# A macaron feed-forward block on one core: parts 1 to 3 of each output product by seven block products, with every instruction of the feed-forwards put in order by a list schedule

## The chip, the core and the metric

The kernel runs on one core of one Trainium2 chip. Its time is the device time of one execution in microseconds (us). TensorE (PE in the profile) multiplies 128x128 weight tiles with 128-row activation tiles into PSUM banks; VectorE (DVE) and ScalarE (ACT) do elementwise work; GpSimd (POOL) and SyncE (SP) mostly start transfers here. Weights come from the chip's memory (HBM) into SBUF by DMA. A transfer that SP starts runs on the profile's queue q1, one that POOL starts on q0.

## What is computed

One decoder block on 512 tokens of width 1024, all in float32: a feed-forward, a token mixer (pooling and dilated attention, gated), a second feed-forward, and a last norm. The change lies in the two feed-forwards:

```python
def swiglu(u, w_in, w_out):
    a, b = jnp.split(u @ w_in, 2, axis=-1)
    return (jax.nn.silu(a) * b) @ w_out
...
u = modulate(rmsnorm(h, g_norm_ffn1[l]), sh1, sc1)
h = h + 0.5 * gt1 * swiglu(u, w_ffn1_in[l], w_ffn1_out[l])
...
u = modulate(rmsnorm(h, g_norm_ffn2[l]), sh3, sc3)
h = h + 0.5 * gt3 * swiglu(u, w_ffn2_in[l], w_ffn2_out[l])
```

The inner width is 2816, that is 22 tiles of 128.

## The kernel before

**Three products for one.** Each float32 operand is split into a high part (rounded to float32r) and a low part (the rest). A product is then three matmuls, high x high, high x low and low x high: `mm3` for 512 token columns, `product` for 256. For a weight tile ACT copies the high part into the ring `whi` (L319) and DVE writes the low part into the ring `wlo` (L336). The rings hold 7 chunks of 1024 columns. `look(4)` lets this splitting run up to four products ahead of PE. For the output weights of the second feed-forward the low part is made otherwise (`added`, L333 and L334): ACT writes minus the high part into `wlo`, and a transfer that POOL starts adds the raw weight to it.

**Pairs.** The feed-forward goes over the 22 inner tiles j. Each needs an a column block and a b column block of w_in, 8 tiles of 128x128 each. The first tiles (6 in feed-forward 1, 4 in feed-forward 2) are done plainly. From there `duo` takes two j at a time by Winograd's form of Strassen's scheme: the product of the 2x2 blocked weights (input halves x a and b) and the 2x2 blocked activations (input halves x token halves) takes seven block products of 24 matmuls with 256 columns, where the plain way takes eight. The weight sums that it needs are four DVE subtractions of 1024 columns to a duo, in `make` (L263). The activation sums are made once for each feed-forward. The end of a duo forms silu(a) times b in `hf` (L776) and splits it into `HI` (ACT) and `HK` (DVE, L783).

**Parts.** The 22 inner tiles are cut into five parts, (0,4), (4,8), (8,12), (12,16), (16,22). After a part's tiles, one duo later for most parts, its output product is added to the residual `H`: 8 output tiles of 128 rows by 512 tokens, each 4 inner tiles by three matmuls of 512 columns (`mm3`, L366 to L368), that is 96 matmuls; then DVE adds gate times bank to `H` (L906, 512 columns, eight times). The last part has six inner tiles and its own code, with the norm behind it.

**What sets the order.** Each engine runs its instructions in the order of the program. That order is written by hand: `look` puts splits and loads ahead of a product, `later` and `step` put DVE and ACT work a product or two behind, `bg` puts one slice of the conditioning product in between (a load of 512 KB and a DVE multiply-accumulate of 1024 columns, L393). Feed-forward 1 carries 32 of these slices, 24 of them beside the outputs of its parts 1 to 3.

Of the kernel before, what the change touches and what calls it, by code (L numbers as in the profile page):

```python
# [18 lines left out]
KT = 8  # L19
# [42 lines left out]

def lay_ffn(w_in, w_out, first, plain):

    ins, outs = [], []
    if first:
        cols = np.concatenate([c for j in range(first) for c in _tiles(j * P, DFF + j * P)])
        for k in range(KT):  # L70
            ins.append(w_in[k * P:(k + 1) * P][:, cols])
    for j in range(first, plain):
        for c in _tiles(j * P, DFF + j * P):
            ins.append(_fmajor(w_in, c))
    for j in range(plain, FT, 2):
        ins.extend(_blocks(w_in, 0, DFF, j))
    for k0, k1 in PARTS:
        for m in range(KT):
            outs.append(_fmajor(w_out[k0 * P:k1 * P], np.arange(m * P, (m + 1) * P)))
    n = KT * (len(PARTS) - 1)  # L80
    return ins, [np.concatenate(outs[i:i + 2], axis=1) for i in range(0, n, 2)] + outs[n:]
# [46 lines left out]
NH = 6  # L128
# [5 lines left out]
def pairs_before(n, part):  # L134

    k1 = PARTS[part][1]
    return k1 if part + 1 == len(PARTS) or (n == 2 and part == 0) else k1 + 2


def chunk_widths():  # L140
    outs = [D] * (KT // 2 * (len(PARTS) - 1)) + [(FT - PARTS[-1][0]) * P] * KT
    f1 = [2 * FIRST * P] * KT + [D] * (2 * (FT - FIRST)), outs
    mix = [D] * 24 + [4 * P] * 2 + ([D] * 4 + [4 * P] * 2) * (KT // 2 - 1) + [D] * KT
    return f1, mix, ([D] * (2 * FT), outs)


class Kernel:
# [6 lines left out]
    def plan(self):  # L154
# [12 lines left out]
        self.shifted, self.added = set(), set()  # L167
# [8 lines left out]
        def blocks(recs):  # L176
            n = len(self.loads)
            self.shifted.update(range(len(self.order), len(self.order) + 7))
            self.loads.extend(recs)
            r11, r12, r22, r21 = (("raw", n + i) for i in range(4))  # L180
            x0, x1 = ("x", 0), ("x", 1)
            for need, src, make in ((0, r11, None), (1, x0, (x0, r12, r11)), (2, x1, (x1, r22, x0)), (3, r21, None),
                                    (3, r12, (r12, r22, r12)), (3, r22, None), (3, x0, (x0, r21, x1))):
                for j, x in enumerate((r11, r12, r22, r21)):
                    if x == src or (make and x in make):
                        self.last[n + j] = len(self.order)
                self.order.append((D, n + need, src, make))
# [5 lines left out]
        def ffn(n, ins, outs, first):  # L193
            j, at = first, 0
            if first:
                plain(ins[:KT])
                at = KT
            for part, (k0, k1) in enumerate(PARTS):
                while j < pairs_before(n, part):
                    if j < PLAIN[n]:  # L200
                        plain(ins[at:at + 2])
                        if n and j < 2:
                            shift(2)
                        j, at = j + 1, at + 2
                    else:
                        blocks(ins[at:at + 4])
                        j, at = j + 2, at + 4
                if n and part + 1 < len(PARTS):
                    self.added.update(range(len(self.order), len(self.order) + KT // 2))
                plain(outs[part * KT // 2:(part + 1) * KT // 2] if part + 1 < len(PARTS) else outs[-KT:])  # L210
# [15 lines left out]
        self.ready = True  # L226
# [30 lines left out]
    def make(self, i):  # L257

        while self.made <= i:
            m = self.order[self.made][3]  # L260
            if m:
                out, x, y = (self.source(z) for z in m)
                self.nc.vector.tensor_tensor(out, x, y, op=OP.subtract)  # L263
            self.made += 1

# [28 lines left out]
    def split_hi(self):  # L294
# [15 lines left out]
        self.make(i)  # L310
        r = self.source(self.order[i][2])
# [32 lines left out]
    def look(self, ahead=3):  # L344

        if self.held is not None:
# [23 lines left out]
    def settle(self, bank, hi, uh):  # L370

        self.nc.tensor.matmul(bank[:, :HT - SHIFT], hi, uh[:, SHIFT:HT], start=True, stop=True, skip_group_check=True)

# [26 lines left out]
    def ada_fin(self, which, j0, j1, g=None):  # L400
# [6 lines left out]
        elif which == "half":  # L407
            nc.vector.tensor_scalar(m, m, 0.5, None, op0=OP.mult)

# [26 lines left out]
    def sumsq(self, m, src):  # L436
# [5 lines left out]
        s = self.tp.tile([P, T], F32, name="ut")  # L442
# [25 lines left out]
    def norm_t(self, n, k, hs):  # L468
        G = self.mod[:, 24 * n + 8 + k:24 * n + 9 + k]
        t = self.tp.tile([P, T], F32, name="ut")  # L470
# [97 lines left out]
    def out_end(self, ms, ksrc, gate):  # L568
# [18 lines left out]
        for h, hs in enumerate((A, Bh)):  # L587
            for m in ms:
# [20 lines left out]
                s = self.tp.tile([P, T], F32, name="ut")[:, :HT]  # L609
# [65 lines left out]

    def ffn_post(self, j, s, pb):
        nc = self.nc
        h = self.fw.tile([P, T], F32, name=("hf", "u3")[j % 2])
        nc.vector.tensor_tensor(h, s, pb, op=OP.mult)
        hh, hl = self.HH[j % NH], self.HL[j % NH]  # L680
        nc.scalar.activation(hh, h, AF.Copy)
        nc.vector.tensor_tensor(hl, h, hh, op=OP.subtract)

    def ffn_silu(self, j, pa):
        s = self.fw.tile([P, T], F32, name=("sl", "u2")[j % 2])
# [22 lines left out]
    def u_steps(self, n):  # L708

        nc, v = self.nc, self.nc.vector  # L710
        (a11, a12), (a21, a22) = self.U4

        def add(o, x, y, op):
            return lambda: v.tensor_tensor(o, x, y, op=op)

        def split(i, u):
            x = u if i < 3 else u.rearrange("p (k t) -> p k t", k=4)
            parts = [lambda: nc.scalar.activation(self.S[i][0], x, AF.Copy),
                     lambda: v.tensor_tensor(self.S[i][1], x, self.S[i][0], op=OP.subtract)]
            return parts if n else lambda: [f() for f in parts]  # L720

        def whole(u, k):
            x = slice(k, k + 4)
            hi, lo = (y.rearrange("p (k t) -> p k t", k=KT)[:, x, :HT] for y in (self.UHv, self.ULv))
            return lambda: v.tensor_tensor(u.rearrange("p (k t) -> p k t", k=4), hi, lo, op=OP.add)

        adds = [add(a22, a21, a22, OP.add), add(a21, a11, a21, OP.subtract), add(a11, a22, a11, OP.subtract),
                add(a12, a12, a11, OP.subtract)]
# [13 lines left out]
    def product(self, bank, u, start, extra=0):  # L742
        M = self.nc.tensor.matmul
        w = self.take()
# [10 lines left out]
    def duo(self, n, j, first, last, extra):  # L755
# [12 lines left out]
        s = self.fw.tile([P, 2 * T], F32, name="sl")  # L768
        c = self.fw.tile([P, 2 * T], F32, name="hf")
        u2, u3, p5 = (self.fw.tile([P, T], F32, name=x) for x in ("u2", "u3", "p5"))  # L770
        q = lambda x: x.rearrange("p (j h t) -> p j h t", j=2, h=2)
        r = lambda x: x.rearrange("p (j t) -> p j t", j=2)
        silu = lambda h, bank: nc.scalar.activation(q(s)[:, :, h, :], r(bank), AF.Silu)

        def mult():
            v.tensor_tensor(c, s, c, op=OP.mult)  # L776

        def high():
            copy(self.HHall[:, j % NH * T:(j % NH + 2) * T], c)

        def low():
            x = slice(j % NH * T, (j % NH + 2) * T)
            v.tensor_tensor(self.HLall[:, x], c, self.HHall[:, x], op=OP.subtract)  # L783


        for i, (bank, u, start) in enumerate(((A, blk(lo4, T1), True), (B, S[0], True), (A, S[1], False),
                                              (C, blk(hi4, T1), False), (A, S[2], False), (B, S[3], False),
                                              (A, blk(hi4, T2), False))):
            if i == 6:
                v.tensor_tensor(q(c)[:, :, 1, :], r(u3), r(p5), op=OP.add)  # L790

# [3 lines left out]
            self.product(bank, u, start, 0 if i else extra)  # L795
            self.step()
# [11 lines left out]
            elif i == 3:  # L808
                silu(0, C)
            elif i == 4:  # L810
                copy(u3, A)
            elif i == 6:
                silu(1, A)
                v.tensor_tensor(q(c)[:, :, 0, :], r(B), r(u2), op=OP.add)
        if last:
            mult()
            high()
            low()
        else:
            self.later(1, mult)  # L820
            self.later(2, high)
            self.later(2, low)

    def ffn2(self):
        self.put, self.now = [], 0
        bk = [self.nb() for _ in range(4)]
        self.head(2, bk, AF.Silu)
# [19 lines left out]
    def open_ffn(self):  # L847
# [3 lines left out]
        self.HHall, self.HLall = (fp.tile([P, NH * T], F32R, name=x) for x in ("HI", "HK"))  # L851
        self.HH, self.HL = ([x[:, i * T:(i + 1) * T] for i in range(NH)] for x in (self.HHall, self.HLall))
# [14 lines left out]
    def ffn(self, n, j, last=None):  # L867

        nc, v = self.nc, self.nc.vector
# [7 lines left out]

        for part, (k0, k1) in enumerate(PARTS):
            tail = part + 1 == len(PARTS)
            extra = 1  # L880
            while j < pairs_before(n, part):
# [3 lines left out]
                else:  # L885
                    self.duo(n, j, last, tail and j + 2 == FT, extra)
                    last, extra = None, 0
                    j += 2
            if n == 0:
                last = self.beside_out(part) or last  # L890
            nk = k1 - k0
            hk = [(self.HH[k % NH], self.HL[k % NH]) for k in range(k0, k1)]
            if not tail:
                for m in range(0, KT, 2):
# [8 lines left out]
                    for i, b in enumerate(bs):  # L903
# [5 lines left out]
                        if n == 0 and part:  # L909
                            self.later((6, 13)[i], self.bg) if m + 2 == KT else self.bg()  # L910
# [39 lines left out]
            else:  # L950
                self.out_tail((4, 5, 6, 7), ks, gate, 1, lambda m: self.X[0][:, m % 2 * HT:])

# [25 lines left out]
    def mix_sums(self, x, slots):  # L978
# [17 lines left out]
        sub = lambda o, y, z: v.tensor_tensor(o, y, z, op=OP.subtract)  # L996

        def last():
# [6 lines left out]
        return [lambda: whole(b, 0, 1), lambda: whole(x[0], 4, 1), lambda: v.tensor_tensor(x[0], x[0], b, op=OP.add),  # L1005
                lambda: whole(x[1], 0, 0), lambda: sub(x[2], x[1], b), lambda: sub(x[1], x[0], x[1]),
                lambda: (hi(0), whole(x[3], 4, 0)), lambda: lo(0), lambda: (hi(1), sub(x[3], x[3], x[1])),
# [421 lines left out]
    def gate_duo(self, s, c, p5, last, rest):  # L1429
# [37 lines left out]
        sig(c, c)  # L1467
# [100 lines left out]
    def build(self):  # L1568
# [3 lines left out]
        self.tp = ctx.enter_context(tc.tile_pool(name="tp", bufs=3))  # L1572
# [18 lines left out]
        self.hpi, self.r4 = tl("hpi", 1), tl("r4", 4)  # L1591
# [6 lines left out]
        tl("pad", 32)  # L1598
        self.tr, self.pi = tl("tr", 5 * P), tl("pi", P, I32)
# [3 lines left out]
        self.todo = []  # L1603
# [197 lines left out]
```

## Time and profile before

| what | value |
|---|---|
| time, median of 3 runs | 993.09 us (993.02 to 994.11) |
| span of the profiled execution | 994.0 us, 0.9 us above the median |
| ACT busy | 490.7 us (49%) |
| POOL busy | 45.6 us (5%) |
| memory read / written | 135.29 MB / 2.24 MB |

From the timeline of PE, feed-forward 1 runs from the start to 355 us, the mixer to about 650 us, feed-forward 2 from there to the end. In feed-forward 1 the outputs of parts 1 to 3 stand at 141 to 163, 201 to 223 and 261 to 283 us; in feed-forward 2 at 770 to 792, 830 to 852 and 890 to 912 us. Between them PE does two duos in 38.1 us. A row of the view by lines names line, engine, operation, output<-inputs, shape and count, then the busy time of the group, the mean ns of one, and the idle time of the engine before it with what ended it. A DVE or ACT instruction's own duration is some 0.08 us longer than the distance to the next one, since the two overlap.

### The profile page before, as it was taken

Reading aid. Unit: us, or ns where it says so; the run is one execution under the profiler, and the core shown is the slowest. Engines: PE = TensorE matmul, PEld = TensorE weight load, DVE = VectorE, ACT = ScalarE, POOL = GpSimd, SP = SyncE. Lnnn points to the kernel's source line nnn. Section 1 sums busy time; section 2 is a strip of 40 time slices with the busy share of each in tenths; the row PEclk is TensorE's granted clock in tenths of the full one; section 3 lists DMA queues with packets and bytes.
Section 4 is the critical chain, followed back from the end, with each engine's and each line's share of the span. In section 5 each row is a group of like instructions: output and inputs, shape, how many; then the busy total and the mean of one; then the engine's idle time right before and its main releaser. Section 6 shows DMA issues by size and latency. Waiting matters only on the chain.

```text
span 994.0 us, 16420 instructions
## 1 busy us (share of the span) xinstructions
PE 983.2 (99%) x6688; PEld 894.6 (90%) x6688; DVE 765.0 (77%) x1072; ACT 490.7 (49%) x730; POOL 45.6 (5%) x49
## 2 busy tenths in 40 slices
PE   9999999999999999999999999999999999999997
PEld 7888999989999899788879998998899898998997
DVE  7989979889797677897988877865695775647753
ACT  5453643625434553455555552555366255363553
POOL 0000000000000000007100000001001001010002
PEclk9999999999999999999999999999999999999999
DMA  9856456464564416664233336416454538264312
GB/s 347 275 196 224 149 149 198 146 196 163 188 189 119 126 56 230 201 200 144 76 106 107 106 121 211 135 44 141 128 177 115 142 118 220 86 151 128 114 33 85
DMA packets 47469, 150.14 MB, mean 151 GB/s; under 512 B 6561, under 2 KB 9377, under 8 KB 47394
## 3 DMA queue, kind: packets, MB, share of 16 engines
q1 hardware_dynamic: 44224, 140.18, 43.3%
q0 software_dynamic: 2592, 8.39, 4.6%
q8 instruction: 52, 0.85, 0.3%
q10 hardware_dynamic: 578, 0.53, 0.2%
q14 instruction: 23, 0.19, 0.1%
HBM read 135.29 MB, written 2.24 MB: 138 GB/s over the span
## 4 chain that ended last, share of the span: by engine, by line
PE 89%; DVE 3%; issue 3%; DMA 3%; SPq 1%; ACT 1%; POOL 0%; POOLq 0%; DVEq 0%; ACTq 0%
PE bank L366 14%; PE bank L368 14%; PE bank L367 14%; PE bank L751 13%; PE bank L753 12%; PE bank L752 12%; PE bank L1727 2%; PE bank L1729 1%; PE bank L1731 1%; DMA wlo<-raw 1%; SPq L1059 1%; PE bank L1403 1%; PE bank L1105 1%; PE bank L1156 1%; PE bank L1404 1%
## 5 line engine op out<-in xcount | busy, mean ns | idle before, releaser
L336 DVE TENSOR_TENSOR wlo<-raw,whi 128x1024 fp32r<-128x1024 f32 (+4 forms) x148 | 155.6, 1064 | 53.9 <-ACT whi L319 53.6
L319 ACT ACTIVATE whi<-raw 128x1024 fp32r<-128x1024 f32 (+4 forms) x162 | 146.4, 921 | 63.1 <-DVE raw L263 51.4
L751 PE MATMUL bank<-UH,whi 128*128 128x256 f32 x640 | 177.1, 277 | 0.0
L752 PE MATMUL bank<-UL,whi 128*128 128x256 f32 x640 | 177.1, 277 | 0.0
L753 PE MATMUL bank<-UH,wlo 128*128 128x256 f32 x640 | 177.1, 277 | 0.0
L366 PE MATMUL bank<-HI,whi 128*128 128x512 f32 (+1 forms) x406 | 146.2, 360 | 0.0
L368 PE MATMUL bank<-HI,wlo 128*128 128x512 f32 (+1 forms) x406 | 145.9, 359 | 0.3 <-DMA wlo<-raw 0.3
L367 PE MATMUL bank<-HK,whi 128*128 128x512 f32 (+1 forms) x406 | 145.9, 359 | 0.0
L336 DVE TENSOR_TENSOR wlo<-X,whi 128x1024 fp32r<-128x1024 f32 (+3 forms) x100 | 106.8, 1077 | 22.8 <-ACT whi L319 22.3
L753 PEld LDWEIGHTS bank<-UH,wlo 128*128 128x128 f32 x640 | 120.5, 188 | 0.0
L751 PEld LDWEIGHTS bank<-UH,whi 128*128 128x128 f32 x640 | 120.1, 188 | 0.4
L752 PEld LDWEIGHTS bank<-UL,whi 128*128 128x128 f32 x640 | 120.2, 188 | 0.0
L319 ACT ACTIVATE whi<-X 128x1024 fp32r<-128x1024 f32 (+3 forms) x104 | 96.2, 944 | 45.9 <-DVE X L263 44.5
L751 PE MATMUL bank<-SH,whi 128*128 128x256 f32 x408 | 113.1, 277 | 0.1
L752 PE MATMUL bank<-SL,whi 128*128 128x256 f32 x408 | 112.9, 277 | 0.0
L753 PE MATMUL bank<-SH,wlo 128*128 128x256 f32 x408 | 112.9, 277 | 0.0
L366 PE MATMUL bank<-UH,whi 128*128 128x512 f32 (+1 forms) x304 | 105.6, 347 | 0.0
L367 PE MATMUL bank<-UL,whi 128*128 128x512 f32 (+1 forms) x304 | 104.2, 343 | 0.1
L368 PE MATMUL bank<-UH,wlo 128*128 128x512 f32 (+1 forms) x304 | 104.0, 342 | 0.0
L368 PEld LDWEIGHTS bank<-HI,wlo 128*128 128x128 f32 x406 | 76.2, 188 | 12.4 <-DMA wlo<-raw 0.7
L366 PEld LDWEIGHTS bank<-HI,whi 128*128 128x128 f32 x406 | 76.2, 188 | 11.4
L367 PEld LDWEIGHTS bank<-HK,whi 128*128 128x128 f32 x406 | 76.3, 188 | 11.3
(349 smaller groups left out, 1870.2 us busy)
## 6 DMA issues: line engine op xcount, KB each, us to landing
raw<-wmix SPq DMA_DIRECT2D x44, 512.0 KB, 3.7
raw<-wf1i SPq DMA_DIRECT2D x31, 512.0 KB, 5.0
raw<-wf2i SPq DMA_DIRECT2D x30, 512.0 KB, 4.4
ada<-wada SPq DMA_DIRECT2D x23, 512.0 KB, 5.2
AR<-wada SPq DMA_DIRECT2D x19, 512.0 KB, 4.3
X<-wf2i SPq DMA_DIRECT2D x14, 512.0 KB, 4.5
cs<-wada SPq DMA_DIRECT2D x12, 512.0 KB, 3.6
X<-wf1i SPq DMA_DIRECT2D x12, 512.0 KB, 4.4
```

The lines of the kernel that those rows point to most:

```text
L319: self.nc.scalar.activation(self.hi[:, y], r[:, x], AF.Copy)
L336: self.nc.vector.tensor_tensor(self.lo[:, y], r[:, x], self.hi[:, y], op=OP.subtract)
L366: M(ps, hi, uh, start=start, stop=False)
L367: M(ps, hi, ul, start=False, stop=False)
L368: M(ps, lo, uh, start=False, stop=stop)
L751: M(o, hi, uh, start=start and p == 0 and k == 0, stop=False, skip_group_check=True)
L752: M(o, hi, ul, start=False, stop=False, skip_group_check=True)
L753: M(o, lo, uh, start=False, stop=k == 3, skip_group_check=True)
L1059: nc.sync.dma_start(w[32 * o:32 * o + 32], t[32 * i:32 * i + 32])
L1105: nc.tensor.matmul(S[:, o], q[:, toks], k[:, ks], start=True, stop=True, skip_group_check=True)
L1156: self.nc.tensor.matmul(self.bO[64 * h:64 * h + 64, P * hp:P * hp + P], x, pt[:, (2 * h + j) * P:(2 * h + j + 1) * P], start=j == first, s ...
L1727: M(b, hi, self.UH[k], start=k == 0, stop=False)
```

## The change

**Seven block products for the outputs.** `_out_blocks` lays the output weights of parts 1 to 3 as four chunks of 2x2 blocks (two inner tiles by two output tiles, two of each side by side). `out_block` multiplies them with the part's h by seven block products of 24 matmuls with 256 columns. A part's last duo and its output are interleaved: six of the duo's products, half of output block 0, the duo's seventh, then the rest.

**The h blocks.** `split_a` and `split_s` make, for each duo in a part from 1 to 3, the four sums of h blocks and split seven blocks of 256 columns (as 512, 256 and 1024 columns) where one split of 1024 columns stood.

**Weight blocks only added.** Signs move into the activations, so that a group of four weight chunks needs additions alone: two on DVE (`make`) and two by transfers that POOL starts (`sum`). This holds for the 17 duos of the feed-forwards, the 3 of the mixer's gates and the 6 outputs. The low parts of three of an output's seven weight operands come by such transfers too (`ADDED`), now in both feed-forwards; in feed-forward 2 the four of part 0 stay as they were.

**Order.** A `Recorder` takes down what both feed-forwards issue and `flush` puts it out again in the order of a list schedule with a cost for each instruction and transfer. PE's own order stays that of the code. The conditioning slices now stand two to a duo and three to an output. Recorded instructions carry line 318 in the changed program.

```diff
+    def sum(self, i):
+        if i in self.merges:
+            out, x = (self.source(z) for z in self.merges.pop(i))
+            self.nc.gpsimd.dma_start(out, x, accum_op=OP.add)
...
-            for need, src, make in ((0, r11, None), (1, x0, (x0, r12, r11)), (2, x1, (x1, r22, x0)), (3, r21, None),
-                                    (3, r12, (r12, r22, r12)), (3, r22, None), (3, x0, (x0, r21, x1))):
+            return n, [(D, n, r11, None), (D, n + 1, x0, (x0, r12, r11)), (D, n + 2, x1, (x1, r22, x0)), (D, n + 3, r21, None),
+                       (D, n + 3, r12, None), (D, n + 3, r22, None), (D, n + 3, x1, None)]
...
+                if i in (2, 3):
+                    self.merges[at] = (("raw", n + 1), ("raw", n + 2)) if i == 2 else (("x", 1), ("raw", n + 3))
...
-                self.nc.vector.tensor_tensor(out, x, y, op=OP.subtract)
+                self.nc.vector.tensor_tensor(out, x, y, op=OP.add)
...
+    def split_s(self, j):
+        v = self.nc.vector
+        a11, a21, a12, a22 = (self.c[:, i * HT:(i + 1) * HT] for i in range(4))
+        s2, s3, s4, s1 = (self.cS[:, i * HT:(i + 1) * HT] for i in range(4, 8))
+        v.tensor_tensor(s1, a22, a21, op=OP.subtract)
+        v.scalar_tensor_tensor(s2, a11, -1.0, s1, op0=OP.mult, op1=OP.subtract)
+        v.tensor_tensor(s3, a11, a21, op=OP.subtract)
+        v.scalar_tensor_tensor(s4, a12, -1.0, s2, op0=OP.mult, op1=OP.subtract)
+        for i0, i1 in ((6, 7), (2, 6)):
+            hi, lo = self.block(j, i0, i1)
+            x = self.cS[:, (i0 + 1) * HT:(i1 + 1) * HT]
+            self.nc.scalar.activation(hi, x, AF.Copy)
+            v.tensor_tensor(lo, x, hi, op=OP.subtract)
...
+        def rest(end):
+            self.look(3)
+            w[1] = self.take()
+            for g in range(2):
+                products(1, g, (0,), True)
+            end()
+            for i in range(2):
+                for g in range(2):
+                    products(i, g, (1,), False)
+                    copy(*((C[g], A[g]), (p5[g], B[g]))[i])
+                    self.step()
...
+            for i in range(2, 7):
+                self.look(4)
+                w[i] = self.take()
+                for g in range(2):
+                    products(i, g, (0, 1), False)
```

Where it moves instructions: DVE, feed-forward 1, from the last steps of a part's second duo into the part's output. Before (part 1; `wlo<-X` and `wlo<-raw` are low parts of weights, `hf` and `HK` the products h and their low parts, `cs` and `AR` the conditioning slices):

```order
L906 SCALAR_TENSOR_TENSOR H<-bank_91,mod,H 128x512
L393 SCALAR_TENSOR_TENSOR AR,mod<-AR,cond 128x1024
L776 TENSOR_TENSOR hf<-sl,hf 128x1024
L263 TENSOR_TENSOR X<-raw_67,X 128x1024
L336 TENSOR_TENSOR wlo<-X,whi 128x256
L336 TENSOR_TENSOR wlo<-X,whi 128x768
L906 SCALAR_TENSOR_TENSOR H<-bank_92,mod,H 128x512
L393 SCALAR_TENSOR_TENSOR cs,mod<-cs,cond 128x1024
L906 SCALAR_TENSOR_TENSOR H<-bank_93,mod,H 128x512
L393 SCALAR_TENSOR_TENSOR AR,mod<-AR,cond 128x1024
L783 TENSOR_TENSOR HK<-hf,HI 128x1024
```

The same place in the changed program (part 2):

```order
L318 TENSOR_TENSOR HK<-hf,HI 128x512
L318 TENSOR_TENSOR hf<-hf,bank_92 128x2x256
L318 TENSOR_TENSOR hf<-hf 128x256
L318 SCALAR_TENSOR_TENSOR hf<-hf 128x256
L318 TENSOR_TENSOR hf<-hf 128x256
L318 SCALAR_TENSOR_TENSOR hf<-hf 128x256
L318 TENSOR_TENSOR HK<-hf,HI 128x256
L318 TENSOR_TENSOR HK<-hf,HI 128x1024
L318 TENSOR_TENSOR X<-raw_65,raw_64 128x1024
L318 TENSOR_TENSOR wlo<-X,whi 128x1024
L318 SCALAR_TENSOR_TENSOR cs,mod<-cs,cond 128x1024
L318 TENSOR_TENSOR wlo<-raw_64,whi 128x1024
```

The product h, its four sums and their low parts now stand in one run between the duo's seventh product and the output, where `hf` and `HK` stood apart, a product or more behind, with other work in between.

POOL, from its first instructions into feed-forward 1. Before, nothing stands there until the mixer's pooling:

```order
L1792 MEMSET const-uint8-127 128x1
L1797 UNCONDITIONAL_BRANCH
L1222 MEMSET tr 128x16
L1229 ISA
L1229 TENSOR_TENSOR rt_4180<-tr 128x527
```

And now (`raw_65<-raw_63` and `X<-X` are the sums of weight chunks, `wlo` the low parts):

```order
L2160 UNCONDITIONAL_BRANCH
L318 DMA raw_65<-raw_63 128x1024
L318 DMA X<-X 128x1024
L318 DMA wlo<-raw_64 128x1024
L318 DMA wlo<-X 128x1024
L318 DMA raw_65<-X 128x1024
L318 DMA wlo<-X 128x256
L318 DMA wlo<-X 128x768
L318 DMA X<-X 128x1024
```

Each of these is issued in this order and waits for its operands before the next is issued; 34 of them stand in feed-forward 1, where there were none, 37 in feed-forward 2, where there were 18, and 6 in the mixer.

More of the change, by code (lines that the diff above doesn't have):

```diff
@@ L672, in head, with plain_of, begin, end @@
         self.held = None
+    def plain_of(self, j):
+        k0, k1 = next(x for i, x in enumerate(PARTS) if x[0] <= j < x[1] and i not in BLOCKED)
+        x = slice(NB + (j - k0) * T if k1 < FT else (j - k0) * T, NB + (j - k0 + 1) * T if k1 < FT else (j - k0 + 1) * T)
+        return self.HI[:, x], self.HK[:, x]
+    def begin(self):
+        self.whole, self.nc = self.nc, Recorder(self.nc, self.before)
+    def end(self):
+        self.nc.flush()
+        self.before = self.nc.before
+        self.nc = self.whole
@@ L740, in later, with product @@
         self.put.append((self.now + n, f))
-    def product(self, bank, u, start, extra=0):
+    def product(self, bank, u, start, extra=0, before=lambda: None):
         M = self.nc.tensor.matmul
+        before()
         w = self.take()
@@ L794, in duo @@
                 self.look(4)
[L795 to L796 removed]
+            if i == 5:
+                v.tensor_tensor(q(c, 1), r(u3), r(p5), op=OP.add)
+                nc.scalar.activation(q(c, 1), q(c, 1), AF.Silu, scale=-1.0)
+            if i == 6 and out:
+                self.product(bank, u, start, 0, out[0])
+            else:
+                self.product(bank, u, start, 0 if i else extra)
             if i == 0:
```

424 lines of the change are left out of this document (348 added, 76 removed).

## The prediction, made before the changed kernel ran

> **What bounds the kernel now.** I read the first page, then the chain of waits, then PE's timeline, then stretches of the two feed-forwards.
>
> ```profile
> span 994.0 us, 16420 instructions
> PE 983.2 (99%) x6688; PEld 894.6 (90%) x6688; DVE 765.0 (77%) x1072; ACT 490.7 (49%) x730; POOL 45.6 (5%) x49
> PE 89%; DVE 3%; issue 3%; DMA 3%; SPq 1%; ACT 1%; POOL 0%; POOLq 0%; DVEq 0%; ACTq 0%
> ```
>
> The last row is the chain: 89% of it is matmul. A busy PE need not be a PE at its pace, so the starts of matmuls are compared, in an output part and in a duo:
>
> ```profile
> 159.76 0.39 PE L367 MATMUL bank<-HK,whi 128*128 128x512 f32 x1
> ...
> 162.71 0.39 PE L368 MATMUL bank<-HI,wlo 128*128 128x512 f32 x1
> ...
> 109.76 0.28 PE L753 MATMUL bank<-SH,wlo 128*128 128x256 f32 x1
> ...
> 112.70 0.28 PE L752 MATMUL bank<-UL,whi 128*128 128x256 f32 x1
> ```
>
> The first two rows are 13 matmuls apart: 0.227 us each with 512 columns. The other two are 26 apart: 0.113 us with 256. Half the columns take half the time. So in the feed-forwards PE runs at its own pace; only fewer columns can shorten them, as long as the other engines keep up. Whether they can is read from the stretches (each a part: two duos and an output; columns are length, then busy us and count of PE, PEld, DVE, ACT, POOL, then clock, DMA share, GB/s):
>
> ```profile
> 163.00:223.00 60.00, 60.00 (x435) 56.24 (x434) 52.77 (x67) 26.71 (x34) 0.00 (x0) 1.00 0.54 175
> 223.00:283.00 60.00, 60.00 (x435) 56.24 (x434) 53.12 (x69) 27.73 (x38) 0.00 (x0) 1.00 0.54 176
> 830.30:890.30 60.00, 60.00 (x436) 56.24 (x435) 38.61 (x40) 30.88 (x40) 4.08 (x6) 1.00 0.50 140
> ```
>
> PE fills all three. In feed-forward 1 DVE has only 7 us free in 60, in feed-forward 2 21 us.
>
> **Matmuls: -16.3 us.** Each of six outputs loses 96 matmuls of 512 columns and gains 168 of 256, by the order 576 and 1008 in all. The 1008 count as 504 full ones: 72 x 0.227 = 16.3 us, half of it in each feed-forward. A part's floor falls from 60.0 to 57.3 us.
>
> **DVE in feed-forward 1: +3 us.** Work per part, from these durations, each less the 0.08 us that overlaps the next:
>
> ```profile
> 211.21 1.22 DVE L263 TENSOR_TENSOR X<-X 128x1024 f32<-128x1024 f32 x1
> 212.34 1.22 DVE L336 TENSOR_TENSOR wlo<-X,whi 128x1024 fp32r<-128x1024 f32 x1
> 213.48 0.74 DVE L906 SCALAR_TENSOR_TENSOR H<-bank,mod,H 128x512 f32<-128x512 f32 x1
> 214.14 1.22 DVE L393 SCALAR_TENSOR_TENSOR cs<-cs,cond 128x1024 f32<-128x1024 f32 x1
> ...
> L790 DVE TENSOR_TENSOR hf<-u,p 128x512 f32<-128x512 f32 x17 | 11.7, 686 | 17.7 <-ACT u L758 17.7
> L336 DVE TENSOR_TENSOR wlo<-raw,whi 128x256 fp32r<-128x256 f32 x8 | 3.4, 419 | 0.8 <-ACT whi L319 0.7
> L520 DVE SCALAR_TENSOR_TENSOR H<-bank,mod,H 128x256 f32<-128x256 f32 x24 | 11.6, 482 | 8.1 <-PE bank L368 8.0
> ```
>
> So 1024 columns occupy 1.14 us, 512 from a bank with the gate 0.66, 512 otherwise 0.60, 256 0.34, or 0.40 from a bank. Per part: weight sums, eight before, six now (four of the duos, two of the output): -2.3. Low parts: 18 before, 21 now less three by transfer: 0. Each duo's end was two of 1024 (2.3) and is three of 512, five of 256 and one of 1024 (4.6): +4.7 for two. The output's eight updates of 512 (5.3) become four additions of 512, eight updates of 256 and four of 512 (8.2): +3.0. One conditioning slice fewer: -1.1. Sum +4.3: about 57 us of DVE work against 57.3 us of PE. Before, DVE idled 7 us a part behind ACT, banks and loads; now there is no room for it. What hides the shortfall is the lead: splits may run four products ahead, 4 x 24 x 0.113 = 10.9 us. Feed-forward 1 has 2.7 such parts (part 1 has a single duo of its kind). If the schedule leaves 3.6 us of idling a part, 2.7 x 3.4 = 9 us are short and the lead covers them, in all but the places where it runs out: I take 3. If idling stays at 7, 18 us are short, 8 beyond the lead; if none is left, 0. Feed-forward 2 carries no slices: 38.6 + 4.3 + 1.1 = 44 of 57, nothing there.
>
> ACT gains three splits, three copies and the smaller pieces, some 12 us a part on 28: hidden by its 30 free.
>
> **DMA engines: +1 us.** What a sum by transfer costs is shown by the second feed-forward, in the share of the queues and in two bursts of four:
>
> ```profile
> q1 hardware_dynamic: 44224, 140.18, 43.3%
> q0 software_dynamic: 2592, 8.39, 4.6%
> ...
> 824.00:839.50 15.50, 15.50 (x98) 13.92 (x98) 7.96 (x10) 9.46 (x12) 2.61 (x3) 1.00 1.01 236
> 884.00:899.50 15.50, 15.50 (x98) 13.92 (x98) 6.19 (x7) 8.97 (x12) 3.48 (x4) 1.00 1.01 230
> ```
>
> A load of 0.524 MB takes 0.433 x 994 x 0.524 / 140.18 = 1.61 us of all 16 engines, a sum 0.046 x 994 x 0.524 / 8.39 = 2.86 us, and in the bursts the engines are full. A part of feed-forward 1 had 0.54 x 60 = 32.4 us of transfers. Now one slice fewer (-1.6) and nine sums (six of chunks, three low parts: +25.7): 56.5 of 57.3 us. Feed-forward 2: 30 - 4 x 2.86 + 25.7 = 44. So in feed-forward 1 two engines are full at once. Bounds: 0 if the order spreads the sums, and 2.7 x 2 = 5 us if each part ends 2 us late because the engines are never quite full. I take 1, near the burst rows, where PE lost nothing.
>
> The Trainium skill (DMA: Bandwidth & Descriptors, Anatomy of one DMA, SWDGE path) fits such a transfer as 2.0 us fixed plus bytes over 436 GB/s, that is 1.2 us of moving for 0.524 MB; by it 28 transfers a part would be an estimated 34 us, and the term 0. The rows above say 56, and they decide.
>
> **The hand-over to an output: +2.4 us.** The first two output blocks need the sum s1 of the last duo's h, 24 matmuls (2.7 us) behind that duo's seventh product. In DVE's order stand the product (0.69 with its end), four sums (4 x 0.34), then the low part of s1 (0.42): 2.5 us if DVE is free. It rarely is: half of a 1.14 us instruction in the way makes 3.1. The low parts of s2 to s4 wait for ACT as well:
>
> ```profile
> L319 ACT ACTIVATE whi<-raw 128x1024 fp32r<-128x1024 f32 x22 | 23.1, 1053 | 13.7 <-DVE raw L263 13.5 <-DMA raw<-wf1i 0.2
> ```
>
> 0.69 + 1.36 + 1.05 + 1.22 = 4.3 us against 39 matmuls, 4.4: no better. So 0.4 us at each of six hand-overs; 0 if DVE is free, 1.1 behind a whole instruction.
>
> **The start of feed-forward 2: -1 us.** There PE waits for a residual update that DVE does late:
>
> ```profile
> 709.07 0.39 PE L368 MATMUL bank<-HI,wlo 128*128 128x512 f32 x1
> 710.49 0.35 PE L372 MATMUL bank<-UH,whi 128*128 128x240 f32 x1 [1.03 <-DVE H L906]
> ```
>
> 1.42 us between starts instead of 0.23: 1.2 lost. The stretch is scheduled anew; four sums of part 0 remain. Between 0 and -1.2, I take -1. In the mixer six sums move to transfers where POOL has finished its pooling: 0.
>
> **Sum:** 994.0 - 16.3 + 3 + 1 + 2.4 - 1 = 983.1 us of span. The median of the runs lies 0.9 below the span: **982 us**.
>
> **Rivals.**
> *DVE bounds feed-forward 1.* The 7 us of idling stay, and the 8 us beyond the lead are lost, which is that feed-forward's whole gain: 982.2 + 5 = 987. For it: 57 of 57. Against it: the lists put DVE's waiting work where its operands are due.
> *The whole gain.* No hand-over, DVE or DMA loss: 994.0 - 16.3 - 1.2 - 0.9 = 975.6. It asks of DVE what it never did in feed-forward 1.
> *Sums land late, slower.* The seventh operand of a group is the third one plus a chunk, summed in place by a transfer that may start only when the third is split. Its way is issue, landing, ACT, DVE:
>
> ```profile
> 822.57 0.86 POOL L334 DMA_DIRECT2D wlo<-raw  x1 [50.90 <-PE bank L752]
> DMA to landing us min/median/max: 4.5/5.6/10.0
> ```
>
> 0.86 + 5.6 + 1.05 + 1.22 = 8.7 us at the median against four products, 10.9; with a landing of 10.0 it is 13.1 and 2.2 us are missing, if the lead is gone. Past a landing of 7.8 us without lead it decides, for 23 groups (17 duos, 6 outputs). At half of them, 11 x 2.2 = 24 us: 994.0 - 16.3 + 24 - 0.9 = 1001. For it: engines at 56.5 of 57.3, where landings lengthen, and POOL's queue, in which one sum that waits holds up the next. Against it: the lead, and that in the bursts PE went on.
> *The change does less than it says* is out for PE, whose counts are in the order; blocks of 256 columns already run at 0.113.
>
> **How the numbers follow.** Changes under 0.2% (2 us) can't be told from none. The forecast, 977 to 986 on its own, has 0.50; DVE as the bound 0.17, a fifth of it within 2 us of before; the whole gain 0.09; late sums 0.24, of which 0.02 end within 2 us. Faster: 0.50 + 0.14 + 0.09 = 0.73; same 0.05; slower 0.22. The range runs from 975, just under the whole gain, to 996, which leaves out most of the late sums (0.17) and little below.
>
> **What would show it.** PE: 57.3 us from one output's end to the next in feed-forward 2, and 57.3 to 59 in feed-forward 1; gaps of 0.2 to 1 us before the first or second output block. DVE above 54 us in such a stretch of feed-forward 1 and near 44 in feed-forward 2; DMA share above 0.9 against 0.8. PE waits on `wlo` or `whi` in rows of tenths of a us for the forecast. If PE's waits lead back to `X<-X` or `raw<-raw` transfers and there are many above 2 us, late sums are right. If feed-forward 1 gains nothing while feed-forward 2 gains 8, DVE or the DMA engines were the bound, and which, their shares tell. If the time is above 995, my reading of the lead as cover is wrong.

## The result: 1005.3 us, 1.2% slower

The changed kernel takes 1005.26 us (median of 4 runs, 1004.15 to 1006.32); the kernel before, timed again beside it, 993.35 us (993.02 to 994.11). The ratio is 1.0115 (0.95 interval 1.0097 to 1.0132). The prediction said 982 us, between 975 and 996.

The first page of the changed kernel, the rows that answer to those shown of before:

```profile
span 1004.4 us, 17772 instructions
...
PE 987.7 (98%) x7120; PEld 917.4 (91%) x7120; DVE 797.4 (79%) x1194; ACT 552.9 (55%) x827; POOL 96.4 (10%) x108
...
q1 hardware_dynamic: 44224, 140.18, 42.1%
q0 software_dynamic: 11088, 38.80, 20.5%
...
PE 81%; DVE 8%; DMA 4%; issue 3%; ACT 2%; SPq 1%; POOL 0%; POOLq 0%; DVEq 0%; ACTq 0%
```

PE is still busy 98% of a longer span: 4.5 us more, though it has 16.3 us less to do at the old pace. So the matmuls themselves have become slower. In PE's timeline of the second feed-forward, the first two rows (an output block) are 27 matmuls apart, and so are the last two (a duo):

```profile
770.02 0.28 PE L318 MATMUL bank<-HI,whi 128*128 128x256 f32 x1
...
773.21 0.28 PE L318 MATMUL bank<-HI,whi 128*128 128x256 f32 x1
```

```profile
797.94 0.28 PE L318 MATMUL bank<-UH,whi 128*128 128x256 f32 x1
...
801.00 0.28 PE L318 MATMUL bank<-UH,whi 128*128 128x256 f32 x1
```

A matmul of 256 columns with activations from `HI` and `HK` starts every 3.19 / 27 = 0.118 us, one with activations from `UH` and `UL` every 0.113 us. The same form, the same weights' ring, the same granted clock of 1.00 (below). In the kernel before, `HI` and `HK` ran at 0.227 for 512 columns, the same as 0.113 for 256. Each row below is one part, two duos and an output, the first of feed-forward 1, the second of feed-forward 2 (columns as in the stretches of the prediction):

```profile
210.10:271.90 61.80, 59.92 (x507) 59.31 (x506) 56.66 (x78) 39.62 (x57) 9.56 (x11) 1.00 0.88 233
...
841.71:900.98 59.27, 59.27 (x508) 59.09 (x507) 49.18 (x66) 39.27 (x53) 7.82 (x9) 1.00 0.75 187
```

Where 57.3 us was forecast, feed-forward 2 takes 59.3, with PE busy all of it. Of the 9.8 us that PE waits in the whole span, 6.5 lie in feed-forward 1 (the view of waits from 85 to 365 us: total, times, longest):

```profile
PE bank L318 <- ACT bank L318: 4.7, 2, 4.4
PE bank L318 <- DVE H L318: 1.5, 1, 1.5
PE bank L318 <- DVE HK L318: 0.3, 1, 0.3
```

To put sizes to both, I took every pair of neighbouring matmuls of 256 or 512 columns and what lay between their starts beyond 0.1134 us per 256 columns. Up to 0.012 us each is called pitch, more is called a gap (waits, and matmuls at half clock):

| us in the profiled execution | before | after |
|---|---|---|
| matmuls at 0.1134 us, against before | 0 | -16.3 |
| pitch | 3.3 | 20.9 |
| gaps | 12.2 | 21.1 |
| span | 994.0 | 1004.4 |

-16.3 + 17.6 + 8.9 = +10.2, and the span grew by 10.4.

**The one large gap** is the first duo of feed-forward 1. POOL's timeline, ACT's, PE's, and two stretches behind the wait (PE's granted clock is the third figure from the right):

```profile
100.35 0.99 POOL L318 DMA_DIRECT2D raw<-raw  x1 [99.90 <-DVE X L318]
```

```profile
109.78 1.06 ACT L318 ACTIVATE whi<-raw 128x1024 fp32r<-128x1024 f32 x1 [3.00 <-DMA raw<-raw]
...
113.59 0.57 ACT L318 ACTIVATE bank<-bank 128x512 f32<-128x512 f32 x1
```

```profile
114.22 0.38 PE L318 MATMUL bank<-SH,whi 128*128 128x256 f32 x1 [4.39 <-ACT bank L318]
```

```profile
114.20:118.50 4.30, 4.28 (x23) 4.29 (x24) 4.09 (x12) 0.48 (x1) 0.64 (x1) 0.61 1.06 262
118.56:125.00 6.44, 6.44 (x58) 6.44 (x57) 6.37 (x10) 5.27 (x7) 0.86 (x1) 1.00 0.97 348
```

A transfer that adds one weight chunk to another is issued at 100.35, and ACT can make the high part of that sum only at 109.78, 9.4 us later. Behind it in ACT's queue stand three more pieces of splits and then the bank copy that PE needs now, at 113.59. PE waits 4.4 us. Then its clock is 0.61 for 4.3 us, in which 23 matmuls run where 38 would: 1.7 us more are lost to the same wait.

### The profile page after: what moved, and what is told of

It is laid out like the page before. It is cut to its first block, busy times and chain, and to the rows that moved or that the text cites. A ratio compares the mean times of both kernels' runs of the same rounds, so it can differ in the third digit from the quotient of the medians.

```text
span 1004.4 us, 17772 instructions
## 1 busy us (share of the span) xinstructions
PE 987.7 (98%) x7120; PEld 917.4 (91%) x7120; DVE 797.4 (79%) x1194; ACT 552.9 (55%) x827; POOL 96.4 (10%) x108
## 4 chain that ended last, share of the span: by engine, by line
PE 81%; DVE 8%; DMA 4%; issue 3%; ACT 2%; SPq 1%; POOL 0%; POOLq 0%; DVEq 0%; ACTq 0%
PE bank L318 51%; PE bank L566 6%; PE bank L567 6%; PE bank L568 6%; DMA raw<-raw 2%; PE bank L1011 2%; PE bank L1013 2%; PE bank L1012 2%; DVE ada L597 2%; DMA ada<-wada 1%; DVE wlo L536 1%; DVE wlo L318 1%; PE bank L1468 1%; PE bank L1766 1%; PE bank L1519 1%
## 5 line engine op out<-in xcount | busy, mean ns | idle before, releaser
L318 PE MATMUL bank<-UH,whi 128*128 128x256 f32 (+2 forms) x680 | 194.8, 288 | 0.0
L318 PE MATMUL bank<-UL,whi 128*128 128x256 f32 (+1 forms) x672 | 193.7, 288 | 0.2 <-DVE UL L702 0.2
L318 PE MATMUL bank<-UH,wlo 128*128 128x256 f32 (+1 forms) x672 | 193.3, 288 | 0.0
L318 PE MATMUL bank<-HI,wlo 128*128 128x256 f32 (+1 forms) x472 | 142.7, 302 | 1.5 <-DVE H L318 1.5
L318 PE MATMUL bank<-HK,whi 128*128 128x256 f32 (+1 forms) x472 | 143.5, 304 | 0.4 <-DVE HK L318 0.3
L318 PE MATMUL bank<-HI,whi 128*128 128x256 f32 (+2 forms) x473 | 143.0, 303 | 0.3 <-ACT bank L318 0.3
L318 DVE TENSOR_TENSOR wlo<-X,whi 128x1024 fp32r<-128x1024 f32 (+2 forms) x111 | 124.0, 1130 | 22.0 <-ACT whi L318 21.6
L318 ACT ACTIVATE whi<-raw 128x1024 fp32r<-128x1024 f32 (+3 forms) x94 | 82.1, 883 | 41.5 <-PE bank L318 31.4
L318 DVE TENSOR_TENSOR wlo<-raw,whi 128x1024 fp32r<-128x1024 f32 (+3 forms) x79 | 77.7, 992 | 10.1 <-ACT whi L318 9.9
L318 PEld LDWEIGHTS bank<-SL,whi 128*128 128x128 f32 x408 | 77.6, 190 | 0.0
```

What stands on the lines that cost most here:

```text
L318: getattr(self.real[eng], method)(*a, **k)
```

## Experiments

**Why the pitch differs.** The change adds a tile of 8 floats, `ng`, ahead of most others. It moves every tile behind it (`HI`, `HK`, the activation sums `SH` and `SL`, `X`, the mixer's tiles) by 32 bytes per partition; `whi`, `wlo`, `UH` and `UL` stand before it and stay. The moved tiles are the ones with the longer pitch. Four runs move tiles and change nothing else. The first gives the 32 bytes back in the changed kernel, the second moves the same tiles of the kernel before by 32 bytes:

```diff
 e1_align (after)
-        tl("pad", 32)
+        tl("pad", 24)
 e2_before_shift (before)
-        tl("pad", 32)
+        tl("pad", 40)
```

> The changed kernel with the spacer behind cs cut from 32 to 24 floats, so that every tile behind it starts 32 bytes lower, on the same multiple of 64 bytes as before the change. Theory A (the small tile ng moved all later tiles by 32 bytes, and matmuls that read their activations from them run at 117 ns instead of 113 per 256 columns): the pitch goes back to 113 everywhere, the 17.6 us of it are gained, span near 987, ratio to before about 0.994. Rival B (late sums by transfer and the order are the whole loss): no change, 1003 to 1007, ratio 1.01.

> The kernel before with the same spacer grown from 32 to 40 floats, so that all tiles behind it start 32 bytes later; nothing else is changed. Theory A: the matmuls on HI, HK, SH, SL and the mixer's tiles go from 113 to 117 ns per 256 columns (227 to 234 per 512), some 15 us: 1006 to 1010, ratio 1.013 to 1.017. Rival B: 993, ratio 1.000.

Measured: e1 998.35 us (996.33 to 999.33), ratio 1.0038 (1.0026 to 1.0050). e2 1011.31 us (1010.75 to 1012.38), ratio 1.0174 (1.0161 to 1.0187): 17 us from 32 bytes of unused space. The output of part 2 in e2, eight matmuls between the rows:

```profile
800.02 0.40 PE L366 MATMUL bank<-HI,whi 128*128 128x512 f32 x1
...
801.88 0.40 PE L368 MATMUL bank<-HI,wlo 128*128 128x512 f32 x1
```

1.86 / 8 = 0.233 us for 512 columns in place of 0.227. So the place of a tile sets the pitch. But e1 is only 7 us faster than the changed kernel, where theory A expected 18, and its trace still has 9.5 us of pitch. The other two move the tiles of the changed kernel by 64 bytes from their place in the kernel before, and the rings by 32 with all else by 64:

```diff
 e3_shift64 (after)
-        tl("pad", 32)
+        tl("pad", 40)
 e5_ring32 (after)
+        tl("padr", 8)
         self.hi, self.lo = tl("whi", RING, F32R), tl("wlo", RING, F32R)
+        tl("pads", 8)
...
-        tl("pad", 32)
+        tl("pad", 24)
```

> The changed kernel with the spacer at 40 floats: the later tiles start 64 bytes above their places of before. Theory A1 (the activation's own address must be a multiple of 64 bytes): as with the spacer of 24, near 987. Theory A2 (what counts is its place against the weights of the same matmul, modulo 256 bytes): not as with 24; pitch above 113 in at least some stages, 990 to 1005. Rival B: 1005.

> The changed kernel with the spacer of 24 and the two weight rings started 32 bytes later (spacers of 8 floats ahead of and behind them, so that UH, UL and all later tiles stay on multiples of 64 bytes). Theory A1 (only the activation's address counts): as with the spacer alone, near 987. Theory A2 (the place of the activation against the weights counts): the pitch rises for all products, UH and UL too, 117 per 256 columns: 1010 to 1020. Rival B: 1005.

Measured: e3 1006.42 us (1006.26 to 1007.66), ratio 1.0127 (1.0113 to 1.0140); e5 1015.55 us (1014.72 to 1016.80), ratio 1.0217 (1.0204 to 1.0230), where `UH` is at 0.118 too. In e3's trace a matmul with `HI` starts every 0.120 us and one with `UH` every 0.113. A multiple of 64 bytes is not enough, and moving the ring by 32 bytes does the same harm as moving the activations.

**The rest of the pitch: a matmul that sets the pace.** In e1 four long stretches of the longer pitch begin at one kind of place (150, 271, 777 and 836 us), and two of them end at one (210 and 896 us). Here is the end of an output and the start of a duo (rows of 240 columns are `settle`, L372 in the kernel before; the row counts it with the next matmul):

```profile
775.87 0.28 PE L318 MATMUL bank<-HI,whi 128*128 128x256 f32 x1
...
777.12 0.28 PE L318 MATMUL bank<-HI,wlo 128*128 128x256 f32 x1
777.23 0.39 PE L318 MATMUL bank<-UH,whi 128*128 128x240 f32 x2
777.46 0.28 PE L318 MATMUL bank<-UL,whi 128*128 128x256 f32 x1
...
780.41 0.28 PE L318 MATMUL bank<-SH,wlo 128*128 128x256 f32 x1
```

0.1136 us over the 11 starts ahead of it, 0.118 over the 25 behind it, and it stays so for 374 matmuls. In the kernel before the weights of an output and of a duo lie 64 bytes apart in the ring (`shifted`), and `settle` stands where that changes. In the changed kernel a blocked output is shifted as the duos are; nothing changes there, and `settle` stayed. e4 leaves it out there, e12 leaves it out of the kernel before, where the place does change. What `settle` writes is overwritten by the product behind it:

```diff
 e4_no_settle (e1)
-            extra = 1
+            extra = int(part - 1 not in BLOCKED)
 e12_before_no_settle (before)
-        if extra:
-            self.settle(bank, w[0][0], self.UH[0])
```

> The kernel with its later tiles back at the place they had before (998.35 us), and the 240-column matmul at the head of a duo left out where that duo follows a blocked output (parts 2, 3 and 4; three places in each feed-forward). Its trace shows that matmul turning the pitch from 113 to 118 ns per 256 columns at 150, 271, 777 and 836 us and from 118 to 113 at 210 and 897 us, for a whole duo pair each time. Theory B (the matmul shifts the phase between the weights' reads and the activations' reads, and is right only where the weights' own place in the ring changes, as it did before between an output and a duo): without it the pitch stays as it was across these places, at 113 for most of both feed-forwards; of the 6 us of pitch that the 998 us kernel has more than the kernel before, 4 to 6 come back: 992 to 995 us. Rival (the pitch follows from which tiles are read, and the matmul only happens to stand there): within 1 us of 998.

> The kernel before without the 240-column matmul at the head of its duos (where the weights' place in the ring does change between output and duo). Theory B (that matmul sets the phase): the duos run at 117 to 118 ns per 256 columns in place of 113, eight stretches of 168 to 336 matmuls, 8 x 1.0 to 1.5 us = 8 to 12 us slower, near 1003 us. Rival (the matmul does nothing for the pace): 0 to 1 us faster, its own 0.1 us for each.

Measured: e4 990.97 us (990.39 to 992.53), ratio 0.9968 (0.9957 to 0.9980), faster than both kernels. e12 1006.06 us (1005.79 to 1006.32), ratio 1.0122 (1.0107 to 1.0137). The same place in e4 (23 starts apart), and in e12 (8 starts in the output, 28 in the duo):

```profile
773.49 0.28 PE L318 MATMUL bank<-UH,whi 128*128 128x256 f32 x1
...
776.09 0.28 PE L318 MATMUL bank<-UH,wlo 128*128 128x256 f32 x1
```

```profile
795.58 0.39 PE L366 MATMUL bank<-HI,whi 128*128 128x512 f32 x1
...
797.39 0.39 PE L368 MATMUL bank<-HI,wlo 128*128 128x512 f32 x1
797.61 0.28 PE L749 MATMUL bank<-UH,whi 128*128 128x256 f32 x1
...
800.91 0.28 PE L750 MATMUL bank<-SL,whi 128*128 128x256 f32 x1
```

0.113 in e4; in e12 0.226 in the output and 0.118 in the duo. e12 came out as expected: the matmul is worth 12 us where the place in the ring changes. In e4 the pace no longer turns where the matmul stood, as expected, but the time fell by more, 7.4 us. In the profiled executions 3.6 us of that are pitch, and they lie in feed-forward 2; the rest is gaps, 4.2 us fewer of them in feed-forward 1. That the matmul caused these too isn't shown.

**Absolute or relative place.** Two runs move the rings and everything behind them together:

```diff
 e14_all_by_64, e15_all_by_32 (e4)
+        tl("padr", 16)        (8 in e15)
         self.hi, self.lo = tl("whi", RING, F32R), tl("wlo", RING, F32R)
```

> The 991 us kernel with the rings of weights and every tile behind them 64 bytes further on, so that each stands to the others as before. If only the place of activations relative to the weights' ring sets the pitch: 113 ns per 256 columns as in that kernel, 990 to 993 us. If an address of its own does (192 past a multiple of 256, as in the 1006 us run with the later tiles alone moved by 64): near 117 ns for those tiles, 1000 us or more.

> The same with 32 bytes in place of 64. If only the relative place counts: 990 to 993 us. If tiles must begin at a multiple of 64 bytes: every product at 117 ns, as in the run with the rings moved by 32, 1005 us or more.

Measured: e14 992.21 us (989.42 to 996.54), e15 992.40 us (986.33 to 995.53). For these two shifts, only the place of the activations relative to the weights counts. These two also show how wide e4's program spreads: with the same relative places it runs from 986 to 997 us. A gap too can turn the pace (in e4's trace at 197 us, behind a gap of 0.7 us, to 0.118 for 445 matmuls), and e15's profiled execution, 3.4 us longer than e14's, holds 4.3 us more pitch.

**Feed-forward 1.** e4 does a part of feed-forward 2 in 57.6 us, but feed-forward 1 still loses:

```profile
148.12:206.93 58.81, 58.20 (x506) 57.74 (x505) 55.17 (x77) 39.65 (x55) 9.07 (x11) 1.00 0.91 241
206.93:268.48 61.55, 60.16 (x506) 59.50 (x505) 57.72 (x82) 39.06 (x56) 8.70 (x11) 1.00 0.91 247
773.49:831.09 57.60, 57.55 (x507) 57.29 (x505) 48.96 (x66) 39.16 (x53) 7.84 (x9) 1.00 0.76 193
```

Is it DVE, the DMA engines, or the order? Each run starts from e4. e6 makes the first group's two sums on DVE, e13 all sums of feed-forward 1; e7 is e6 with the outputs' low parts of feed-forward 1 on DVE; e8 is e6 without the list schedule.

```diff
 e6_first_sum_dve, e13_sums_dve (e4)
             out, x = (self.source(z) for z in self.merges.pop(i))
+            if i in self.early:
+                self.nc.vector.tensor_tensor(out, out, x, op=OP.add)
+                return
             self.nc.gpsimd.dma_start(out, x, accum_op=OP.add)
...
+        self.early = set(sorted(self.merges)[:2])      (e13: {i for i in self.merges if i < base})
 e7_low_parts_dve (e6)
-ADDED = {0: (0, 3, 5), 2: (0, 3, 5)}
+ADDED = {0: (), 2: (0, 3, 5)}
 e8_as_recorded (e6)
-        for i in order:
+        for i in range(N):
```

> The same kernel without those matmuls, and the two sums of the very first group of weights in feed-forward 1 made by DVE in place of transfers. Theory C (the one large stall of feed-forward 1, 5.1 us at 108 us and then 5.5 us at half pace, is a bank copy standing on ACT behind the high part of a sum whose transfer took 9 us to land): both go, 7.5 us less than without this edit, about 986 us. Rival (PE was only early there, and the time would be lost a little later to DVE, which gets two instructions of 1.2 us more where it has no room): 0 to 3 us less.

> The kernel with both edits, and in feed-forward 1 the three low parts of an output by DVE instead of transfers (nine transfers of 2.9 us of the DMA engines fewer, nine DVE instructions of 1.14 us more, and nine ACT copies fewer). If the DMA engines are what makes sums land late at the hand-overs of feed-forward 1 (252 to 262 us): 2 to 4 us faster than the kernel with both edits. If DVE has no room there (the rival of the prediction): 3 to 9 us slower. Within 1 us: neither is full.

> The kernel with both edits, its feed-forwards put out in the order in which they were recorded, without the list schedule. If the schedule is what keeps DVE's and ACT's work where it is due: slower by 10 us or more. If the lead of four products alone covers it: within 3 us.

> The 991 us kernel with all the sums of feed-forward 1 made by DVE, none by transfers (the low parts of the outputs still come by transfers): some 23 transfers of 2.9 us of the DMA engines fewer, 23 DVE instructions of 1.14 us more, 26 us of DVE work in a feed-forward where DVE has little room. If DVE is the bound of feed-forward 1 (the rival of the prediction): 8 to 20 us slower than 991. If late transfers are what costs feed-forward 1 its 6 to 8 us: 2 to 6 us faster. If the two balance: within 2 us.

Measured: e6 992.30 us (986.94 to 996.10); e7 991.20 us (989.89 to 995.39); e13 995.67 us (990.73 to 998.02); e8 1025.68 us (1021.84 to 1028.37). e8 shows what the list schedule is worth, 33 us. Of the other three none is faster than e4, and only e13 can be told from it, some 5 us slower. Feed-forward 1 as a whole in e4 and in e13:

```profile
103.20:361.50 258.30, 252.31 (x2075) 247.62 (x2075) 226.82 (x319) 155.59 (x219) 28.72 (x33) 0.99 0.80 218
```

```profile
103.00:361.80 258.80, 250.68 (x2076) 245.35 (x2075) 248.67 (x340) 157.43 (x218) 10.59 (x12) 0.99 0.59 173
```

With 22 us of work moved from transfers to DVE, the DMA share falls from 0.80 to 0.59 and DVE rises from 88% to 96%. That the two stretches are nearly equally long is chance: by the account above, e13's holds 3.0 us more gaps and 2.5 us less pitch, and it is from the fastest of e13's 12 executions (990.7 us). PE's waits in feed-forward 1, first in e4, then in e13:

```profile
PE bank L318 <- ACT bank L318: 3.8, 1, 3.8
PE bank L318 <- DVE H L318: 1.2, 2, 0.6
PE bank L318 <- DVE HK L318: 0.8, 2, 0.7
```

```profile
PE bank L318 <- DVE HK L318: 3.0, 5, 1.3
PE bank L318 <- ACT bank L318: 2.3, 1, 2.3
PE bank L318 <- DVE H L318: 1.7, 3, 0.6
```

So nothing is gained by sparing the DMA engines at DVE's cost, and PE's waits on DVE grow from 2.0 to 4.7 us. The run falls between the times that its three cases gave, and as it changes both engines at once, it can't say what either costs alone. DVE isn't simply full in e4: 22 us more of work cost only some 5 us, and what PE waits for are single late items. e6 shows this at the place of the large gap. ACT's rows:

```profile
112.63 1.07 ACT L318 ACTIVATE whi<-X 128x1024 fp32r<-128x1024 f32 x1 [2.66 <-DVE X L318]
113.60 0.57 ACT L318 ACTIVATE hf<-bank 128x512 f32<-128x512 f32 x1
```

The bank copy (`hf<-bank`) now stands behind a high part that waits for a weight sum on DVE, and two gaps of 1.8 and 2.2 us stand there in place of one of 4.0: theory C had the place and the queue right, but DVE is as late as the transfer was.

Last, the schedule's own estimate of a landing, with the two edits of e4 (e9) and those of e6 (e11):

```diff
-                fin = server + (3500. if op_add[i] else 1500.)
+                fin = server + (6500. if op_add[i] else 1500.)
```

The time left behind a sum in `total` was raised by the same 3 us.

> The 991 us kernel (tiles back at their place, no 240-column matmul between blocks), with the list schedule told that a sum by transfer lands 6.5 us after its turn at the DMA engines in place of 3.5, since the records show 6.6 to 8 us from issue to landing at the median and 9.4 for the first one. In ACT's order the high parts of sums move behind bank copies and the h splits at some places. Theory C (PE's waits in feed-forward 1 are bank copies and h splits standing on ACT behind a sum that lands later than the schedule thinks): 2 to 6 us faster than 991. Rival (the waits come from too much work at once on DVE and the DMA engines, in whatever order): within 1.5 us of 991.

> The same with the first group's two sums on DVE as well. Theory C: as fast as the longer landing alone or 1 to 4 us faster. Rival: 990 to 994 us, with a wide spread as in the run with the first sums on DVE alone (987 to 996).

Measured: e9 1009.99 us (1007.24 to 1022.08), e11 996.34 us (994.05 to 998.85), neither within the times expected. PE's waits in feed-forward 1 of e9:

```profile
PE bank L318 <- DVE H L318: 5.3, 3, 3.2
PE bank L318 <- DMA wlo<-X: 5.2, 1, 5.2
PE bank L318 <- DVE HK L318: 4.7, 4, 1.7
```

In e4 PE waited 3.8 us there for a bank copy; in e9 1.4 us of that are left, and the rows above hold 15 us of other waits. But this does not test theory C with a truer figure. By the code of `flush`, a sum that finds the DMA engines free lands 0.96 + 1.0 + 2.86 + 3.5 = 8.3 us after its issue, and with 6.5 in place of 3.5 it lands after 11.3. In e4's trace POOL's 77 transfers take 4.5 to 10.6 us from issue to landing, 6.0 at the median. The new figure lies above all of them, the old one above most. What a nearer one would do stays open.

## Why the prediction was wrong

**The step that failed** is the pace of a matmul. The prediction compared 512 and 256 columns, found 0.227 and 0.113, and said that blocks of 256 columns "already run at 0.113"; on this the rival that the change does less than it says was put aside. The pace isn't a property of the form. It depends on where the activations lie against the weights' ring, and on what `settle` was there to set. The change touched both, by a tile of 32 bytes and by shifting the outputs' weights with `settle` left in: 17.6 us of pitch, more than the 16.3 us that it saves. e1 and e4 together take 15.0 of these back. (The other part of the excess, 8.9 us of gaps more than before, is the subject of the terms on feed-forward 1 below.) The trace of before had it in view. Here are two rows from its first duos of feed-forward 2, 26 starts apart, 30 us behind those quoted for the start of that feed-forward:

```profile
739.92 0.28 PE L751 MATMUL bank<-UH,whi 128*128 128x256 f32 x1
...
742.98 0.28 PE L753 MATMUL bank<-SH,wlo 128*128 128x256 f32 x1
```

0.118 us, in the form for which the prediction wrote 0.113. That stretch begins at 722 us, right behind a gap of 0.2 us.

**Matmuls, -16.3 us:** the count is right and the saving is there, once the pitch is. e4's parts of feed-forward 2 take 57.60 us; 504 x 0.1134 = 57.2 was the floor.

**Hand-over, 0.4 us each:** 57.6 - 57.2 = 0.4 in feed-forward 2, as forecast, and in e4's trace it stands where it was forecast, in gaps at the first matmuls with `HI` and `HK` (758, 816 and 874 us). In feed-forward 1 the term was mis-sized: there the gaps at the start of the three outputs (130 to 135, 190 to 197 and 249 to 258 us) are 0.8, 1.3 and 2.3 us. For the longest of them PE waits until 253.99 us for a low part that DVE begins at 252.71, when ACT has made its high part.

**DVE in feed-forward 1 (+3), DMA engines (+1):** mis-sized. From the end of part 0's output to the mixer, e4 takes 258.3 us where before took 251.9 and the forecast was 251.9 - 8.2 + 3 + 1 + 1.2 = 248.9. Beyond the pace, e4's trace holds 15.0 us there, where the forecast had 5.2: pitch 4.6, the first duo's wait 4.0 and the low clock behind it 1.6, other gaps 4.8, none over 0.9 and 4.4 of them at the hand-overs. The DVE work was estimated well (55.2 and 57.7 us busy in parts of 57 forecast). What failed at the first duo is the lead as cover. Splits made ahead stand in ACT's queue in front of the copy that PE needs now; when the operand of one is late, the lead is what holds PE up.

**Start of feed-forward 2 (-1):** the 1.2 us wait ahead of the first duo is gone in the changed kernel, and the mixer with that start takes 354.2 us in e4 for 355.6 before.

**Span to median:** I took 0.9 us off. The changed kernel's median lies 0.9 above the span of its profiled execution: 1.8 us of error in this step.

**The rivals.** *Sums land late* was closest in time (1001) for another reason. Its mechanism is there, with a landing of 9.4 us, but at one place, not at 11. *DVE bounds feed-forward 1* is half right by e4: that feed-forward gains nothing while the other gains all. But e13 puts 22 us more on DVE and is only 4.7 us slower than e4, so a total of busy time isn't the bound. And "if the time is above 995, my reading of the lead is wrong" was no test: most of the excess had another cause.

**Left open:** why the relative place matters, and why 64 bytes for the tiles alone (e3) leave `UH` fast and `HI` slow, though the rings' chunks themselves stand 64 bytes apart without harm. A guess is a phase that `UH` and `HI` would need to share; it wasn't tried. The waits of feed-forward 1 that remain in e4 weren't removed by any run, and why a gap turns the pace in one place and not in another isn't known.

## What to carry to other kernels

Before a saving in matmuls is counted, look whether matmuls of one form start equally far apart in all stages; where they don't, list which tiles they read and where those lie, and count every tile that a change allocates as a part of the change. An instruction that is there only to set the pace goes when the reason for it goes. And a queue that is served in order turns work done early into work in the way, as soon as its operand is late.

## What was not expected of the hardware

- 32 bytes of unused space per partition made a kernel 17 us (1.7%) slower (e2). The same 32 bytes between rings and activations, made by moving the rings, cost 17 us against e1 (e5); moving both together cost nothing (e14 and e15, within 1.5 us of e4).
- One matmul of 240 columns sets the pace of some 340 that follow; taken out of the kernel before, its duos run at 0.118 in place of 0.113 us, 12 us in all (e12).
- After the wait of 4.4 us in the changed kernel PE ran at its full pace for 0.9 us more, and then 15 matmuls of 256 columns at 0.21 us each: the clock fell not at the wait but behind it (the granted clock is 0.50 from 115.1 to 118.5 us). The Trainium skill (TensorE: Matmul & The Clock Gate, Part 1) has the gate judge activity in free-running windows of about 3.4 us; the trace agrees with that in the length, 3.4 us, and in coming late.
